# Small products and transposes of a state space preparation, quad by quad or gathered over two quads

## The chip, the cores and the metric

The kernel runs on one core of a Trainium2 chip. The metric is the device time of one execution in microseconds. An execution under the profiler gives, beside its own time, a span (first to last instruction) and the trace from which all rows below are taken. Engines: TensorE (PE, with PEld for its weight loads), VectorE (DVE), ScalarE (ACT), GpSimd (POOL), SyncE (SP).

## The reference

A trunk of two layers on x (256 positions, 2048 wide). Each layer is a token mixer, a cross-attention to 256 memory rows and a squared-ReLU MLP, all with residual adds. The mixer of layer 0 is a gated MLP, that of layer 1 a diagonal complex state space layer, cut here to what matters:

```python
lam = lax.complex(jnp.minimum(lam_re, LAM_RE_MAX), lam_im)      # 128 groups x 64 states
lam_bar = jnp.exp(lam * jnp.exp(log_dt)[:, None])
b_bar = ((lam_bar - 1.0) / lam)[..., None] * bmat                # 64 x 16 per group
bu = jnp.einsum('gpc,bsgc->sbgp', b_bar, u)
_, states = lax.associative_scan(combine, (a, bu), axis=0)       # a = lam_bar at every position
y = jnp.einsum('gcp,sbgp->bsgc', cmat, states).real + d_skip * u
```

The kernel works on chunks of T = 8 positions. For that it needs, for each group, matrices that depend on the parameters alone: the inputs of a chunk to its last state (P), the state to the outputs (Q), and the inputs to the outputs inside a chunk (K). Preparing these is the work that the change touches.

## The kernel before

**The main work.** Nearly all time is matmuls on weights that stream from memory. Every weight tile of 128 x 1024 fp32 values is loaded by SP (`wraw`, 4 buffers), split by ScalarE into a high part (`whi`, line 101) and by VectorE into the rest (`wlo`, line 102), 3 buffers each, and multiplied by TensorE in three passes. In the first MLP, up-projections (lines 163 and 165, 16 matmuls a tile, four tiles to an output, after which lines 168, 169, 545, 101 and 102 make `r`, `hh` and `hl`) alternate with down-projections (lines 579 to 581, 12 matmuls a tile, eight tiles to an output).

**The side work.** `ssm_prep` (from line 672) puts its work as a list of pieces on `self.side`. `tick`, called once per weight tile, takes the next piece off the list at every second tile while the MLP of layer 0 is traced, and gives it a priority 200 instructions behind the main work. A scheduler then orders each engine's queue by priority and by what is ready; at run time each queue is worked off in that order.

**The preparation.** The 128 groups are worked on in 32 quads of four. Each quad has three pieces: `quad` (line 789) loads `b_bc` into `bcq` (3 buffers) and makes `bb` (2 buffers; lines 800 to 802). `quad_q` makes `qt` (lines 810 to 812, 2 buffers), writes it to Qd, multiplies four products of `bb` and `qt` (line 822: 32 x 128 results into one PSUM tile `kp`), and takes the result through `kd` (2 buffers; ScalarE at line 826, VectorE at 827) to Kd by four DMAs (line 830). `quad_p` makes `pq` (lines 810 to 812, one buffer), transposes it in four 128 x 128 pieces (line 838), copies the result to `po` (ScalarE, line 840) and writes it to Pd (line 841). The four products are given to the scheduler with `high_priority(offset=g)`, which puts them at one priority; the transposes have one after the other. PSUM tiles come from `ps`, which alternates between two pools of two banks.

**Behind it.** The mixer of layer 1 reads Pd, Kd and Qd back (line 865), starting at the end of this MLP. All these DMAs stand in POOL's queue.

Of the kernel before, what the change touches and what calls it, by code (L numbers as in the profile page):

```python
# [9 lines left out]
F32 = mybir.dt.float32  # L10
# [3 lines left out]
ALU = mybir.AluOpType  # L14
AX = mybir.AxisListType

P = 128
# [14 lines left out]
T = 8  # L32
# [6 lines left out]
class Trunk:  # L39
# [632 lines left out]
    def ssm_prep(self, pool):  # L672
# [6 lines left out]
        nc, a = self.nc, self.a  # L679
        v = nc.vector  # L680
        W = [P, P]
        NL = 2 * T - 1
# [7 lines left out]
        dsk = pool.tile([P, G // 4], F32, name="dsk", bufs=1)  # L690
        eye = pool.tile([P, 16], F32, name="eye", bufs=1)
# [3 lines left out]
        e = {}  # L695
# [88 lines left out]
        def cols(q):  # L784

            g0 = 32 * (q // 8) + q % 8
            return slice(g0, g0 + 25, 8)

        def quad(q):
            bcq = pool.tile([P, 4, 4, 16], F32, name="bcq", bufs=3)  # L790
            nc.gpsimd.dma_start(out=bcq, in_=a["b_bc"][q])
            v.tensor_scalar(out=bcq[:, 2:4], in0=bcq[:, 2:4], scalar1=sg[:, 0:1], scalar2=None, op0=ALU.mult)
            B1, C2, B2, C1 = (bcq[:, i] for i in range(4))
            bb = pool.tile([P, 4, 2, 16], F32, name="bb", bufs=2)
            tq = pool.tile([P, 4, T + 1, 16], F32, name="tq")
            tb = tq.rearrange("p a b c -> p (a b c)")[:, 0:64].rearrange("p (a c) -> p a c", a=4)
            f1 = F[:, 0, cols(q)].unsqueeze(2).broadcast_to([P, 4, 16])
            f2 = F[:, 1, cols(q)].unsqueeze(2).broadcast_to([P, 4, 16])
            for k, (x1, x2, op) in enumerate(((B1, B2, ALU.subtract), (B2, B1, ALU.add))):
                v.tensor_tensor(out=bb[:, :, k], in0=f1, in1=x1, op=ALU.mult)  # L800
                v.tensor_tensor(out=tb, in0=f2, in1=x2, op=ALU.mult)
                v.tensor_tensor(out=bb[:, :, k], in0=bb[:, :, k], in1=tb, op=op)
            e[q] = bcq, bb, tq

        def times(out, tmp, n, q, x1, x2):
            t1 = T1[:, 0:n, cols(q)].rearrange("p w g -> p g w").unsqueeze(3).broadcast_to([P, 4, n, 16])
            t2 = T2[:, 0:n, cols(q)].rearrange("p w g -> p g w").unsqueeze(3).broadcast_to([P, 4, n, 16])
            b1 = x1.unsqueeze(2).broadcast_to([P, 4, n, 16])
            b2 = x2.unsqueeze(2).broadcast_to([P, 4, n, 16])
            v.tensor_tensor(out=out, in0=t1, in1=b1, op=ALU.mult)  # L810
            v.tensor_tensor(out=tmp, in0=t2, in1=b2, op=ALU.mult)
            v.tensor_tensor(out=out, in0=out, in1=tmp, op=ALU.subtract)

        def quad_q(q):
            bcq, bb, tq = e[q]
            qt = pool.tile([P, T + 1, 4, 16], F32, name="qt", bufs=2)
            times(qt.rearrange("p w g c -> p g w c"), tq, T + 1, q, bcq[:, 3], bcq[:, 1])
            nc.gpsimd.dma_start(out=self.Qd[q // 2][q % 2].rearrange("p r n -> r p n"), in_=qt[:, 1:])
            kp = self.ps([P, T, 16])
            for g in range(4):  # L820
                with self.tc.high_priority(offset=g):
                    nc.tensor.matmul(kp[32 * g:32 * g + 32], bb[:, g], qt[:, 0:T, g, :], start=True, stop=True,
                                     skip_group_check=True)
            kd = pool.tile([P, NL, 16], F32, name="kd", bufs=2)
            nc.gpsimd.memset(kd[:, 0:T - 1, :], 0.0)
            nc.scalar.copy(out=kd[:, T:, :], in_=kp[:, 1:, :])
            v.scalar_tensor_tensor(out=kd[:, T - 1, :], in0=eye, scalar=dsk[:, q:q + 1], in1=kp[:, 0, :],
                                   op0=ALU.mult, op1=ALU.add)
            for t in range(4):
                nc.gpsimd.dma_start(out=self.Kd[q // 2][:, :, q % 2, t], in_=kd[32 * t:32 * t + 16])  # L830

        def quad_p(q):
            bcq, bb, tq = e.pop(q)
            pq = pool.tile([P, 4, T, 16], F32, name="pq")
            times(pq, tq[:, :, 0:T, :], T, q, bb[:, :, 0], bb[:, :, 1])
            pt = self.ps([P, 4, P])
            for g in range(4):
                nc.tensor.transpose(pt[:, g, :], pq[:, g].rearrange("p j c -> p (j c)"), self.ident)
            po = pool.tile([P, 4, P], F32, name="po", bufs=2)
            nc.scalar.copy(out=po, in_=pt)  # L840
            nc.gpsimd.dma_start(out=self.Pd[q // 2][:, q % 2], in_=po)

        sd = self.side
        sd += [poles, bar, zoh]
# [2 lines left out]
        sd += [lambda k=k: power(k) for k in range(5, T + 1)]  # L847
        sd += [lambda: spread(5), last]
        for q in range(G // 4):
            sd += [lambda q=q: quad(q), lambda q=q: quad_q(q), lambda q=q: quad_p(q)]  # L850


    def s5(self, x, cur, nxt):
# [362 lines left out]
```

## Time and profile before

| what | us |
|---|---|
| median of 3 runs (lowest, highest) | 2852.18 (2847.0, 2854.78) |
| the profiled execution's own time | 2848.29 |
| its span | 2846.5 |
| TensorE busy in the span | 2811.6 |
| VectorE busy | 1830.3 |
| ScalarE busy | 1333.4 |
| first and last product of line 822 start at | 791.8 and 1335.5 |
| first and last transpose of line 838 start at | 799.1 and 1344.3 |

A row of the profile names line, engine, operation, output and inputs, shape and count. Matmuls are pipelined: a row's length is longer than the distance to the next start, so costs are read from starts. The waits say which engine waited for which line, the total, the number and the longest.

### The profile page before, as it was taken

The page shows a single profiled execution, that of the slowest core. Times are in us where ns is not written, and L with a number is a line of the kernel's source. Part 1 is how long each engine was busy: PE and PEld are TensorE (multiplying, and loading weights), DVE is VectorE, ACT ScalarE, POOL GpSimd, SP SyncE. Part 2 cuts the span into 40 slices and gives each one's busy share as a digit, 9 for nine tenths or more (in the row PEclk, how much of TensorE's full clock was granted, in tenths as well). Part 3 has the DMA queues.
Part 4 walks back from the last instruction along what each step waited for, and adds up shares of the span by engine and source line. Part 5 has one row for each costly group of instructions (what it writes and reads, how often), then busy time and mean ns, then how long its engine had stood idle before and what let it go on. Part 6 is the DMA issues. An engine that isn't in the chain of part 4 may idle for free.

```text
span 2846.5 us, 39576 instructions
## 1 busy us (share of the span) xinstructions
PE 2811.6 (99%) x15238; PEld 2359.5 (83%) x15238; DVE 1830.3 (64%) x2548; ACT 1333.4 (47%) x1714; POOL 204.0 (7%) x380
## 2 busy tenths in 40 slices
PE   8999999999999999999999999999999999999998
PEld 6888888888888888888777788888888888888886
DVE  6765655585778788787567666555556555565555
ACT  5445544444544444444465445444454444344443
POOL 1000000000022222222011000000000000000000
PEclk9999999999999999999999999999999999999999
DMA  8766655558677777777879766565556666666665
GB/s 288 215 208 200 193 181 177 168 177 241 189 218 226 217 224 219 218 221 218 230 251 275 218 212 207 171 179 180 177 183 192 192 189 188 193 186 192 191 187 154
DMA packets 180461, 579.55 MB, mean 204 GB/s; under 512 B 37440, under 2 KB 39664, under 8 KB 179504
## 3 DMA queue, kind: packets, MB, share of 16 engines
q1 hardware_dynamic: 141440, 511.77, 59.2%
q0 software_dynamic: 38688, 65.19, 8.6%
q8 instruction: 119, 1.95, 0.3%
q14 instruction: 70, 0.57, 0.1%
q10 hardware_dynamic: 144, 0.07, 0.0%
HBM read 553.88 MB, written 22.94 MB: 203 GB/s over the span
## 4 chain that ended last, share of the span: by engine, by line
PE 92%; DMA 3%; DVE 2%; ACT 1%; issue 1%; SPq 0%; POOL 0%; DVEq 0%; ACTq 0%; POOLq 0%
PE acc L163 25%; PE acc L165 13%; PE acc L146 9%; PE acc L145 9%; PE acc L147 9%; PE acc L581 8%; PE acc L580 8%; PE acc L579 8%; PE ps L515 1%; DMA wraw<-in_f_w_down 1%; PE ps L459 1%; DVE wlo L102 1%; PE ps L214 1%; DMA wraw<-in_b_w_in 1%; DMA wraw<-in_f_w_up 1%
## 5 line engine op out<-in xcount | busy, mean ns | idle before, releaser
L102 DVE TENSOR_TENSOR wlo<-wraw,whi 128x1024 fp32r<-128x1024 f32 x952 | 1162.9, 1223 | 842.2 <-ACT whi L101 840.4
L101 ACT CAST whi<-wraw 128x1024 fp32r<-128x1024 f32 x952 | 1001.0, 1052 | 1297.1 <-PE acc L163 402.6
L163 PE MATMUL acc<-act,whi 128*128 128x512 f32 x3072 | 1081.9, 396 | 1.1 <-ACT whi L101 1.1
L165 PE MATMUL acc<-act,wlo 128*128 128x256 f32 x3072 | 864.4, 281 | 0.8 <-DVE wlo L102 0.8
L163 PEld LDWEIGHTS acc<-act,whi 128*128 128x128 f32 x3072 | 575.9, 187 | 133.7 <-issue 1.6
L165 PEld LDWEIGHTS acc<-act,wlo 128*128 128x128 f32 x3072 | 580.3, 189 | 5.2 <-DVE wlo L102 1.8
L145 PE MATMUL acc<-whi,act 128*128 128x512 f32 x1248 | 490.6, 393 | 8.7 <-ACT whi L101 7.2
L146 PE MATMUL acc<-wlo,act 128*128 128x512 f32 x1248 | 488.6, 392 | 5.5 <-DVE wlo L102 5.5
L147 PE MATMUL acc<-whi,act 128*128 128x512 f32 x1248 | 488.0, 391 | 0.3 <-DVE act L102 0.3
L580 PE MATMUL acc<-wlo,hh 128*128 128x512 f32 x992 | 389.5, 393 | 0.5 <-DVE wlo L102 0.4
L579 PE MATMUL acc<-whi,hh 128*128 128x512 f32 x992 | 388.9, 392 | 0.0
L581 PE MATMUL acc<-whi,hl 128*128 128x512 f32 x992 | 388.7, 392 | 0.0
L145 PEld LDWEIGHTS acc<-whi,act 128*128 128x128 f32 x1248 | 235.0, 188 | 58.1 <-ACT whi L101 7.7
L146 PEld LDWEIGHTS acc<-wlo,act 128*128 128x128 f32 x1248 | 235.1, 188 | 55.3 <-DVE wlo L102 8.2
L147 PEld LDWEIGHTS acc<-whi,act 128*128 128x128 f32 x1248 | 235.2, 188 | 48.4 <-DVE act L102 0.7
L580 PEld LDWEIGHTS acc<-wlo,hh 128*128 128x128 f32 x992 | 186.3, 188 | 42.0 <-DVE wlo L102 2.0
L581 PEld LDWEIGHTS acc<-whi,hl 128*128 128x128 f32 x992 | 186.3, 188 | 40.2 <-issue 1.6
L579 PEld LDWEIGHTS acc<-whi,hh 128*128 128x128 f32 x992 | 186.3, 188 | 39.9 <-issue 0.4
L830 POOL DMA_DIRECT2D Kd<-kd x128 | 72.4, 580 | 178.9 <-issue 166.7
L563 DVE SCALAR_TENSOR_TENSOR x<-acc,r,x 128x512 f32<-128x512 f32 x62 | 43.6, 745 | 8.2 <-PE acc L581 8.1
L176 ACT ACTIVATE junk<-x 128x512 f32<-128x512 f32 x56 | 35.3, 630 | 25.8 <-DVE x L556 13.3
L101 ACT CAST hh<-r 128x512 fp32r<-128x512 f32 x64 | 39.5, 617 | 16.7 <-DVE r L545 16.6
(287 smaller groups left out, 1658.0 us busy)
## 6 DMA issues: line engine op xcount, KB each, us to landing
wraw<-in_f_w_up SPq DMA_DIRECT2D x256, 512.0 KB, 4.2
wraw<-in_f_w_down SPq DMA_DIRECT2D x256, 512.0 KB, 4.2
wraw<-in_a_w_in SPq DMA_DIRECT2D x64, 512.0 KB, 4.4
wraw<-in_x_w_q SPq DMA_DIRECT2D x64, 512.0 KB, 3.7
wraw<-in_x_w_k SPq DMA_DIRECT2D x64, 512.0 KB, 3.6
wraw<-in_x_w_v SPq DMA_DIRECT2D x64, 512.0 KB, 3.7
wraw<-in_x_w_o SPq DMA_DIRECT2D x64, 512.0 KB, 3.7
wraw<-in_b_w_out SPq DMA_DIRECT2D x64, 512.0 KB, 4.4
```

Of the source, the lines that this page charges most:

```text
L101: self.nc.scalar.copy(out=hi, in_=src)
L102: self.nc.vector.tensor_tensor(out=lo, in0=src, in1=hi.bitcast(F32), op=ALU.subtract)
L145: nc.tensor.matmul(out[t], ah[:, kt, sl], hi[:, kk, :], start=st, stop=False)
L146: nc.tensor.matmul(out[t], ah[:, kt, sl], lo[:, kk, :], start=False, stop=False)
L147: nc.tensor.matmul(out[t], al[:, kt, sl], hi[:, kk, :], start=False, stop=en)
L163: nc.tensor.matmul(acc[:, f, :], hi[:, kk, sl], both[:, kt].rearrange("p a s -> p (a s)"), start=st, stop=False, skip_group_check=True)
L165: nc.tensor.matmul(acc[:, f, 0:S], lo[:, kk, sl], ah[:, kt, :], start=False, stop=en, skip_group_check=True)
L563: nc.vector.scalar_tensor_tensor(out=xc, in0=acc[:, t, :], scalar=r2[:, t:t + 1], in1=xc, op0=ALU.mult, op1=ALU.add)
L579: nc.tensor.matmul(acc[:, t, :], ah[:, kt % 4, sl], hi[:, kk, :], start=st, stop=False)
L580: nc.tensor.matmul(acc[:, t, :], ah[:, kt % 4, sl], lo[:, kk, :], start=False, stop=False)
L581: nc.tensor.matmul(acc[:, t, :], al[:, kt % 4, sl], hi[:, kk, :], start=False, stop=en)
L830: nc.gpsimd.dma_start(out=self.Kd[q // 2][:, :, q % 2, t], in_=kd[32 * t:32 * t + 16])
```

## The change

The three pieces of a quad become `quad`, `matrices` (`qt` and its write) and `inputs` (`pq`, now with two buffers). After `inputs` of every second quad the same piece also runs `products` for both quads: eight products into one PSUM tile `kp`, then eight transposes into two, all sixteen at one priority, and then the copies and writes of both quads.

```diff
-        def quad_q(q):
-            bcq, bb, tq = e[q]
+        def matrices(q):
+            bcq, bb, tq = e[q]
             qt = pool.tile([P, T + 1, 4, 16], F32, name="qt", bufs=2)
             times(qt.rearrange("p w g c -> p g w c"), tq, T + 1, q, bcq[:, 3], bcq[:, 1])
             nc.gpsimd.dma_start(out=self.Qd[q // 2][q % 2].rearrange("p r n -> r p n"), in_=qt[:, 1:])
-            kp = self.ps([P, T, 16])
-            for g in range(4):
-                with self.tc.high_priority(offset=g):
-                    nc.tensor.matmul(kp[32 * g:32 * g + 32], bb[:, g], qt[:, 0:T, g, :], start=True, stop=True,
-                                     skip_group_check=True)
...
-        def quad_p(q):
-            bcq, bb, tq = e.pop(q)
-            pq = pool.tile([P, 4, T, 16], F32, name="pq")
+        def inputs(q):
+            bb, tq, qt = e[q]
+            pq = pool.tile([P, 4, T, 16], F32, name="pq", bufs=2)
             times(pq, tq[:, :, 0:T, :], T, q, bb[:, :, 0], bb[:, :, 1])
-            pt = self.ps([P, 4, P])
-            for g in range(4):
-                nc.tensor.transpose(pt[:, g, :], pq[:, g].rearrange("p j c -> p (j c)"), self.ident)
...
+        def products(q0):
+            quads = [(q, *e.pop(q)) for q in (q0, q0 + 1)]
+            kp = self.ps([P, 2, T, 16])
+            pts = [self.ps([P, 4, P]) for _ in quads]
+            n = 0
+            for i, (q, bb, qt, pq) in enumerate(quads):
+                for g in range(4):
+                    with self.tc.high_priority(offset=n):
+                        nc.tensor.matmul(kp[32 * g:32 * g + 32, i], bb[:, g], qt[:, 0:T, g, :], start=i == 0,
+                                         stop=True, skip_group_check=True)
+                    n += 1
+            for (q, bb, qt, pq), pt in zip(quads, pts):
+                for g in range(4):
+                    with self.tc.high_priority(offset=n):
+                        nc.tensor.transpose(pt[:, g, :], pq[:, g].rearrange("p j c -> p (j c)"), self.ident)
+                    n += 1
+            for i, (q, *_) in enumerate(quads):
+                kd = pool.tile([P, NL, 16], F32, name="kd", bufs=2)
+                nc.gpsimd.memset(kd[:, 0:T - 1, :], 0.0)
+                nc.scalar.copy(out=kd[:, T:, :], in_=kp[:, i, 1:, :])
+                v.scalar_tensor_tensor(out=kd[:, T - 1, :], in0=eye, scalar=dsk[:, q:q + 1], in1=kp[:, i, 0, :],
+                                       op0=ALU.mult, op1=ALU.add)
+                for t in range(4):
+                    nc.gpsimd.dma_start(out=self.Kd[q // 2][:, :, q % 2, t], in_=kd[32 * t:32 * t + 16])
+            for (q, *_), pt in zip(quads, pts):
+                po = pool.tile([P, 4, P], F32, name="po", bufs=2)
+                nc.scalar.copy(out=po, in_=pt)
+                nc.gpsimd.dma_start(out=self.Pd[q // 2][:, q % 2], in_=po)
...
-            sd += [lambda q=q: quad(q), lambda q=q: quad_q(q), lambda q=q: quad_p(q)]
+            sd += [lambda q=q: quad(q), lambda q=q: matrices(q), lambda q=q: inputs(q)]
+            if q % 2:
+                last_piece = sd.pop()
+                sd += [lambda q=q, f=last_piece: (f(), products(q - 1))]
```

How the scheduler orders TensorE's queue with this can be read from the built programs. Before, in the second quad (the products of a quad, then its transposes between the down-projection's matmuls):

```order
L580 MATMUL acc_7051<-wlo_7073,hh_5584 128x512
L822 MATMUL ps_6735<-qt_6730,bb_6686 32x128 x4
L581 MATMUL acc_7051<-whi_7072,hl_5585 128x512
...
L579 MATMUL acc_7051<-whi_7120,hh_5911 128x512
L838 MATMUL ps_6788<-ident_84,pq_6784 128x128
L580 MATMUL acc_7051<-wlo_7121,hh_5911 128x512
L838 MATMUL ps_6788<-ident_84,pq_6784 128x128
L581 MATMUL acc_7051<-whi_7120,hl_5912 128x512
```

After, in the fifth pair, at the end of an up-projection (line 837 are the products, 843 the transposes; `bb_7804` and `pq_7912` are of the pair's first quad, `bb_7972` and `pq_8080` of its second):

```order
L843 MATMUL ps_8085<-ident_84,pq_7912 128x128 x4
L165 MATMUL acc_8292<-act_4834,wlo_8373 128x256
L163 MATMUL acc_8292<-act_4834,whi_8372 128x512
...
L837 MATMUL ps_8084<-qt_7863,bb_7804 32x128
L843 MATMUL ps_8086<-ident_84,pq_8080 128x128 x4
L837 MATMUL ps_8084<-qt_7863,bb_7804 32x128 x3
L837 MATMUL ps_8084<-qt_8024,bb_7972 32x128 x4
L579 MATMUL acc_8402<-whi_8405,hh_7447 128x512
```

The first quad's transposes stand in a row; a few large matmuls later come one product, the second quad's transposes in a row, and the other seven products in a row. It is so in all 16 pairs.

VectorE's queue at the same pair, after the change (line 849 is what 827 was; `wlo_8406` and `wlo_8424` belong to the two tiles that TensorE works on behind the pair's products):

```order
L102 TENSOR_TENSOR wlo_8406<-wraw_8403,whi_8405 128x1024 [waits DMAHW1_49,PE_49,Activation_49]
L102 TENSOR_TENSOR wlo_8424<-wraw_8421,whi_8423 128x1024 [waits DMAHW2_49,PE_49,Activation_49]
L800 TENSOR_TENSOR bb_8172<-F_5579,bcq_8169 128x4x16 [waits PE_49]
L800 TENSOR_TENSOR bb_8172<-F_5579,bcq_8169 128x4x16
L102 TENSOR_TENSOR wlo_8487<-wraw_8484,whi_8486 128x1024 [waits DMAHW3_49,Activation_49]
L169 TENSOR_TENSOR r_8291<-acc_8292,r_8291 128x512 [waits Activation_49]
L849 SCALAR_TENSOR_TENSOR kd_8103<-eye_5576,dsk_5575,ps_8084 128x16 [waits DMASW5_49,DMASW0_49,Activation_49]
```

The first operation on the next pair's `bb` waits for TensorE, since its buffer is the one that the products above read; before, it waited for the products of the quad before the last.

ScalarE's queue at that place, after the change (848 is what 826 was, 855 what 840 was):

```order
L101 CAST whi_8486<-wraw_8484 128x1024 [waits DMAHW3_49,DVE_49,PE_49]
L168 COPY r_8291<-acc_8292 128x512 [waits PE_49]
L848 COPY kd_8103<-ps_8084 128x112 [waits DMASW5_49,DMASW6_49,DMASW0_49,DMASW7_49,PE_49,Pool_49]
L855 COPY po_8122<-ps_8086 128x512 [waits DMASW4_49]
L848 COPY kd_8111<-ps_8084 128x112 [waits DMASW2_49,DMASW3_49,DMASW1_49,DMASW4_49,DVE_49,Pool_49]
L101 CAST hh_8185<-r_8291 128x512 [waits DVE_49]
L101 CAST whi_8504<-wraw_8502 128x1024 [waits DMAHW4_49,PE_49,Activation_49]
```

The copies of both quads' `kd` and the second `po` stand together here, and the second copy out of `ps_8084` waits for VectorE; before, one `kd` copy stood here for each quad, out of a bank of its own.

More of the change, by code (lines that the diff above doesn't have):

```diff
@@ L818, in quad_q @@
             nc.gpsimd.dma_start(out=self.Qd[q // 2][q % 2].rearrange("p r n -> r p n"), in_=qt[:, 1:])
-            kp = self.ps([P, T, 16])
-            for g in range(4):
-                with self.tc.high_priority(offset=g):
-                    nc.tensor.matmul(kp[32 * g:32 * g + 32], bb[:, g], qt[:, 0:T, g, :], start=True, stop=True,
-                                     skip_group_check=True)
-            kd = pool.tile([P, NL, 16], F32, name="kd", bufs=2)
-            nc.gpsimd.memset(kd[:, 0:T - 1, :], 0.0)
@@ L826, in quad_q @@
[L826 to L830, printed above, removed]
-        def quad_p(q):
-            bcq, bb, tq = e.pop(q)
-            pq = pool.tile([P, 4, T, 16], F32, name="pq")
-            times(pq, tq[:, :, 0:T, :], T, q, bb[:, :, 0], bb[:, :, 1])
-            pt = self.ps([P, 4, P])
-            for g in range(4):
[L838 to L841, printed above, removed]
+            e[q] = bb, tq, qt
@@ new lines, in inputs @@
+        def inputs(q):
+            bb, tq, qt = e[q]
+            pq = pool.tile([P, 4, T, 16], F32, name="pq", bufs=2)
+            times(pq, tq[:, :, 0:T, :], T, q, bb[:, :, 0], bb[:, :, 1])
+            e[q] = bb, qt, pq
+        def products(q0):
[26 more added lines that the diff above has]
+                nc.gpsimd.dma_start(out=self.Pd[q // 2][:, q % 2], in_=po)
```

## Prediction

> **What bounds the kernel now.** I read the page's first lines, then the chain that ended last, and then the stretch in which the prepared work runs.
>
> ```profile
> span 2846.5 us, 39576 instructions
> PE 2811.6 (99%) x15238; PEld 2359.5 (83%) x15238; DVE 1830.3 (64%) x2548; ACT 1333.4 (47%) x1714; POOL 204.0 (7%) x380
> PE 92%; DMA 3%; DVE 2%; ACT 1%; issue 1%; SPq 0%; POOL 0%; DVEq 0%; ACTq 0%; POOLq 0%
> ...
> 770.00:1345.00 575.00, 575.00 (x3123) 476.23 (x3122) 465.70 (x742) 255.14 (x314) 138.81 (x250) 1.00 0.74 218
> ```
>
> TensorE is on the path 92% of the time. In the stretch of the first MLP that holds all 32 quads (770 to 1345 us; the columns are length, then busy time of PE, weight loads, DVE, ACT, POOL) it is never idle, at a granted clock of 1.00. So an operation there costs what it pushes the next large matmul back. VectorE is busy for 465.7 of 575 us, 81%: it is the engine that could become late. I therefore need two things: the price of small matmuls between large ones, and VectorE's margin.
>
> **What the small work costs now.** The first fence has one quad's products, the second its transposes one by one, the third four transposes in a row (start, length).
>
> ```profile
> 791.23 0.39 PE L579 MATMUL acc<-whi,hh 128*128 128x512 f32 x1
> 791.45 0.39 PE L580 MATMUL acc<-wlo,hh 128*128 128x512 f32 x1
> 791.77 0.43 PE L822 MATMUL ps<-qt,bb 128*32 128x128 f32 x8
> 792.13 0.50 PE L581 MATMUL acc<-whi,hl 128*128 128x512 f32 x1
> 792.46 0.39 PE L579 MATMUL acc<-whi,hh 128*128 128x512 f32 x1
> ```
>
> ```profile
> 819.41 0.39 PE L579 MATMUL acc<-whi,hh 128*128 128x512 f32 x1
> 819.64 0.27 PE L838 MATMUL ps<-ident,pq 128*128 128x128 f32 x1
> 819.67 0.48 PE L580 MATMUL acc<-wlo,hh 128*128 128x512 f32 x1
> ...
> 820.72 0.48 PE L580 MATMUL acc<-wlo,hh 128*128 128x512 f32 x1
> 821.03 0.39 PE L581 MATMUL acc<-whi,hl 128*128 128x512 f32 x1
> 821.26 0.39 PE L579 MATMUL acc<-whi,hh 128*128 128x512 f32 x1
> ```
>
> ```profile
> 868.92 0.39 PE L163 MATMUL acc<-act,whi 128*128 128x512 f32 x1
> 869.15 0.28 PE L165 MATMUL acc<-act,wlo 128*128 128x256 f32 x1
> 869.27 0.60 PE L838 MATMUL ps<-ident,pq 128*128 128x128 f32 x4
> 869.63 0.48 PE L163 MATMUL acc<-act,whi 128*128 128x512 f32 x1
> 869.94 0.28 PE L165 MATMUL acc<-act,wlo 128*128 128x256 f32 x1
> ```
>
> Large matmuls start 0.227 us apart (791.23 to 791.45, less rounding). From 791.45 to 792.46 there are two such steps, 0.454, but 1.01 us passed: a quad's products cost 0.556 us. The four are eight rows, since each fp32 product takes two passes. Most of the price is not work: the first product starts 0.32 us behind a large matmul instead of 0.227, and the last of the eight (start 791.77 + 0.43 - 0.27, its own length) is followed only 0.20 us later by a large one, which then takes a step of 0.33 instead of 0.227.
>
> Four single transposes: 819.41 to 821.26 is 1.85 us for six large steps (1.362), so 0.49 us. Four in a row: 869.15 to 869.94 is 0.79 us for steps of 0.117 and 0.230, so 0.44 us. The trace has both kinds and mixtures; I take the middle, 0.465. In all: 32 x 0.556 + 32 x 0.465 = 17.8 + 14.9 = 32.7 us.
>
> **What they cost after the change.** The order shows, in each of the 16 pairs of quads, four transposes in a row, some large matmuls, and then one block: one product, four transposes, seven products. The products are not in one run; the lone one costs a change of shape into and out of the transposes. The prices of such changes stand in the later state space stage (L919, L967, L973 are products on 32 columns, L935 transposes):
>
> ```profile
> 1458.11 1.88 PE ps L919 x64
> ...
> 1492.81 1.09 PE L935 MATMUL ps<-ident,z 128*128 128x128 f32 x8
> 1493.66 0.47 PE L145 MATMUL acc<-whi,act 128*128 128x512 f32 x1
> ...
> 1528.42 1.03 PE L935 MATMUL ps<-ident,z 128*128 128x128 f32 x8
> 1529.38 0.64 PE L967 MATMUL ps<-dq,us 128*32 128x128 f32 x16
> ```
>
> 64 rows in 1.88 us are sixteen passes of four: (1.88 - 0.27) / 15 = 0.107 us a pass. Eight transposes behind other transposes need 7 x 0.109 to their last start (869.27 to 869.63 gives that step), so from 1528.42 the last starts at 1529.18 and the product 0.20 later. Behind products, 1492.81 to 1493.66 is 0.85 where seven steps and the 0.03 to the large matmul are 0.79: the first step there takes 0.06 more. Products to transposes I take as products to a large matmul, 0.20.
>
> The block, from the start of the last large matmul ahead to the second one behind: 0.32 in; 0.13 for the lone product's two passes (0.16 for four products, less three issue steps); 0.20 to the transposes; 0.38 for their steps (0.166 + 2 x 0.109); 0.20 back; 0.37 for seven products (0.16 + 2 x 0.107); 0.20 out; 0.33 for the first large step. Together 2.13, less the two ordinary steps 0.454: 1.68 us. With the other four transposes, 0.44, a pair costs 2.12 us; now it costs 2 x (0.556 + 0.465) = 2.04. So **+0.08 us a pair, +1.3 us in all**. The bounds: if the lone product with its two changes (0.13 + 0.20 + 0.06) cost nothing, 16 x (0.08 - 0.39) = -5 us; if the two changes at the transposes each cost as much as one to a large matmul and back (0.09 + 0.11 more), 16 x 0.28 = +4.5 us. I take +1.3, since each step in it has a row.
>
> **VectorE and ScalarE.** The elementwise work is the same in number and size; it moves. These are the waits in the stretch, then the groups that VectorE's queue is made of:
>
> ```profile
> DVE wlo L102 <- ACT whi L101: 59.6, 54, 1.9
> DVE bcq L792 <- DMA bcq<-in_b_bc: 24.1, 17, 4.0
> DVE pq L810 <- PE ps L838: 9.9, 13, 1.1
> DVE bb L800 <- PE ps L822: 8.2, 12, 1.2
> ...
> PEld acc L165 <- DVE wlo L102: 0.6, 2, 0.3
> ```
>
> ```profile
> L102 DVE TENSOR_TENSOR wlo<-wraw,whi 128x1024 fp32r<-128x1024 f32 x197 | 240.2, 1220 | 60.2 <-ACT whi L101 59.6
> L811 DVE TENSOR_TENSOR tq<-T,bcq 128x576 f32<-128x576 f32 x32 | 24.2, 757 | 0.9
> L812 DVE TENSOR_TENSOR qt<-qt,tq 128x576 f32<-128x576 f32 x32 | 24.1, 754 | 0.5
> L810 DVE TENSOR_TENSOR pq<-T,bb 128x512 f32<-128x512 f32 x32 | 22.0, 687 | 9.9 <-PE ps L838 9.9
> ```
>
> VectorE waits for TensorE in two places now (9.9 and 8.2 us) and for the b_bc loads (24.1 us, once 4.0), and TensorE paid only 0.6 us for all of it, because its weights are two to three tiles ahead. With a second pq buffer the 9.9 us can go: worth nothing, as nobody waited. The bb wait grows: the first bb of a pair overwrites a buffer that all products of the pair before have to have read, and in VectorE's queue it stands behind two splits that TensorE has not used yet. Behind the wait comes a whole pair's work. In the up-projection, from the bb wait to the end of the sixth split behind it, I count 6 splits at 1.14 (their spacing; the group's mean is 1.22, with overlap), 4 operations at 0.75, 4 at 0.69, 11 small ones at 0.22, two quick ones on kd and six on r and hl at 0.6: 19.1 us. TensorE needs that split seven tiles after the block; a tile is 8 x (0.230 + 0.117) = 2.78 us, so 19.4 us. It is a tie with 0.3 us to spare in perhaps half of the pairs; in the down-projection there is less elementwise work and some 1.5 us to spare. I cost it at nothing, with bounds of 0 and, if VectorE's work comes out 5 to 10% longer (1 to 2 us, less the 0.3), 8 x 0.7 to 8 x 1.7 = 6 to 14 us.
>
> The later Kd and Pd writes are the same in number; now ten of them are issued together. Behind the last ones on POOL stand the first loads of the state space stage:
>
> ```profile
> 1337.72 2.27 POOL L830 DMA_DIRECT2D Kd<-kd  x4 [12.11 <-DVE kd L827]
> 1345.66 0.57 POOL L841 DMA_DIRECT2D Pd<-po  x1 [5.67 <-ACT po L840]
> 1346.21 2.13 POOL L865 DMA_DIRECT2D pq<-Pd  x4
> ```
>
> Eight Kd issues at 0.57 us push these loads back by about 5 us; their first use is the L919 row at 1458, so this costs nothing.
>
> **Forecast.** 2848.29 us (span 2846.5 and 1.8 around it) + 1.3 = 2849.6 for a run like the profiled one. That one lies 3.9 us under the median shown; against the median it is 2852.18 + 1.3 = **2853.5 us**, no measurable change.
>
> **Rivals.**
> *Faster: the products run together.* If the lone product joins the other seven, a pair needs one block of products (0.556 + 2 x 0.107 = 0.77) and two runs of transposes (0.88): 1.65 instead of 2.04, 16 x -0.39 = -6 us, 2846 us. That is what the change says it does. The order of TensorE's rows speaks against it in every pair. Beyond 0.3% (8.6 us, about what a measurement of this kernel tells from no change) it would also need idle time to vanish, of which there is hardly any. 5%.
>
> *Slower: the splits come late behind the block.* Both quads' products now lie in one PSUM bank. ScalarE copies the first half, VectorE reads it, and only then ScalarE may copy the second half; the next tile's cast stands behind that copy. VectorE reaches its read after the bb work, a split and an operation on r: 0.35 + 1.14 + 0.6 + 0.2 = 2.3 us. Then copy, hh and cast (0.25 + 0.62 + 1.05) bring whi to 4.2 us and, in VectorE's queue, wlo to some 6.3 us, needed at three tiles, 8.2. So it decides only when 1.9 us are lost there, or 0.3 us at the sixth split. A loss of 1 to 1.5 us in half of the pairs is 8 to 12 us: 2862 to 2865. For it speaks the tie; against it that VectorE lost 4 us at once before and TensorE lost 0.3. 17%.
>
> The Trainium skill (PSUM — Partial Sum Buffer, section on PSUM bank collisions) says that two engines must not be in one bank and 32-partition quadrant at the same time, and that software therefore orders ScalarE against VectorE too. By that rule the hand-over just described is there and is all of this rival's first part; without it the second copy would follow the first at once and the forecast would lose this rival, not a microsecond of its sum. The trace of before has a bank per quad, so no row here shows it.
>
> **Chances and range.** Same (within 0.3%) 0.78, slower 0.17, faster 0.05. The range takes in the -5 of the bounds with the spread of the runs shown (2847.0 to 2854.78) and reaches up to the slower case: 2846 to 2864.
>
> **What would show it.** Right: in the timeline of a pair four transposes, then one product row of two, four transposes, and fourteen rows of products, with 1.6 to 1.75 us lost; products and transposes together near 34 us. Wrong on TensorE: a lone product with no gap to the transposes. Wrong on VectorE: waits of the weight loads for wlo of more than a few us in all, at 860 to 960 us or 1045 to 1140 us above all; or b_bc waits longer than 4 us.

## The result and the profile after

The changed kernel takes 2884.94 us (median of 5, 2880.08 to 2888.72) against 2850.17 for the kernel before (median of 5): a ratio of 1.0122, with a 95% interval of 1.011 to 1.0135. It is 35 us slower, where 2853.5 was forecast, and outside the stated range.

First the lines of the page after that answer to those of before, then the row of the windows for 770 to 1345 us (its columns are explained in the prediction):

```profile
span 2878.3 us, 39497 instructions
PE 2821.2 (98%) x15238; PEld 2370.9 (82%) x15238; DVE 1817.8 (63%) x2548; ACT 1336.1 (46%) x1714; POOL 202.8 (7%) x380
...
770.00:1345.00 575.00, 551.18 (x2927) 458.61 (x2927) 425.85 (x702) 241.22 (x294) 126.76 (x231) 0.98 0.68 206
```

The span is 31.8 us longer. In the stretch in which TensorE was never idle, it is now busy for 551.2 of 575 us, and its granted clock is 0.98 instead of 1.00. VectorE did not become the fuller engine: 425.9 us instead of 465.7, with 702 of its operations in the stretch instead of 742. So something makes both wait. The waits of 770 to 1400 us name it:

```profile
DVE bcq L792 <- DMA bcq<-in_b_bc: 60.4, 16, 7.1
...
DVE bb L800 <- PE ps L837: 17.7, 9, 2.4
...
PE acc L165 <- DVE wlo L102: 15.5, 5, 3.7
...
ACT kd L848 <- DVE kd L849: 10.5, 11, 1.4
...
PE acc L580 <- DVE wlo L102: 8.3, 2, 4.6
```

VectorE's wait for the `b_bc` load grew from 24.1 to 60.4 us, the longest from 4.0 to 7.1; and TensorE, which had lost 0.6 us to `wlo` between 770 and 1345 us, now waits seven times between 1.9 and 4.6 us. One of the seven, engine by engine. TensorE (line 580 needs the `wlo` of its tile):

```profile
836.87 0.39 PE L579 MATMUL acc<-whi,hh 128*128 128x512 f32 x1
841.86 0.80 PE L580 MATMUL acc<-wlo,hh 128*128 128x512 f32 x1 [4.60 <-DVE wlo L102]
842.45 0.63 PE L581 MATMUL acc<-whi,hl 128*128 128x512 f32 x1
842.88 0.63 PE L579 MATMUL acc<-whi,hh 128*128 128x512 f32 x1
```

VectorE, with that `wlo` in its last row:

```profile
832.41 0.22 DVE L802 TENSOR_TENSOR bb<-bb,tq 128x64 f32<-128x64 f32 x1
839.72 0.29 DVE L792 TENSOR_SCALAR bcq<-bcq,sg 128x128 f32<-128x128 f32 x1 [7.09 <-DMA bcq<-in_b_bc]
...
840.59 1.22 DVE L102 TENSOR_TENSOR wlo<-wraw,whi 128x1024 fp32r<-128x1024 f32 x1
```

GpSimd, which issues the load (the bracket is its idle time before the row):

```profile
818.99 0.57 POOL L856 DMA_DIRECT2D Pd<-po  x1 [32.95 <-ACT po L855]
821.07 0.55 POOL L856 DMA_DIRECT2D Pd<-po  x1 [1.51 <-ACT kd L848]
822.69 4.53 POOL L852 DMA_DIRECT2D Kd<-kd  x8 [1.07 <-issue]
827.14 0.90 POOL L819 DMA_DIRECT2D Qd<-qt  x1
...
828.10 0.65 POOL L791 DMA_DIRECT2D bcq<-in_b_bc  x1
```

Read from the bottom up: the load is issued at 828.10, and VectorE's first use of it starts at 839.72, 11.6 us later. Ahead of it stand ten stores (two of Pd, eight of Kd) and then, with only a memset between it and the load, the write of Qd. VectorE works its queue off in order, so the split of `wlo` at 840.59 stands behind that first use. The rows of the kernel before have the load ahead of Qd:

```profile
804.72 0.54 POOL L791 DMA_DIRECT2D bcq<-in_b_bc  x1 [2.83 <-DVE tq L811]
806.53 0.85 POOL L818 DMA_DIRECT2D Qd<-qt  x1 [1.27 <-DVE qt L812]
```

What each place costs stands in the table of DMA issues for 770 to 1345 us (the last number is the median from issue to landing); the kernel before, then after:

```profile
Qd<-qt POOLq DMA_DIRECT2D x32, 256.0 KB, 12.1
...
bcq<-in_b_bc POOLq DMA_DIRECT2D x29, 128.0 KB, 3.3
```

```profile
Qd<-qt POOLq DMA_DIRECT2D x30, 256.0 KB, 11.9
...
bcq<-in_b_bc POOLq DMA_DIRECT2D x29, 128.0 KB, 5.8
```

A write of Qd takes 12 us in both kernels. Before, every load was issued 0.5 to 2.8 us ahead of the next write of Qd, and none of the 29 took more than 5.0 us. After, 11 of the 29 were issued 0.9 to 1.0 us behind one; these took 10.6 to 12.6 us, and each landed 0.2 to 0.8 us after that write. In three pairs of the same trace the ten stores stand ahead of the load and Qd behind it (the loads at 974.54, 1018.68 and 1244.39); these loads took 3.9, 4.1 and 4.8 us. The first of them, with its Qd issued only at 977.27:

```profile
969.84 4.62 POOL L852 DMA_DIRECT2D Kd<-kd  x8 [1.00 <-DVE r L545]
...
974.54 0.65 POOL L791 DMA_DIRECT2D bcq<-in_b_bc  x1
```

So the stores alone do not make a load late; the write of Qd does.

**The account of the 31.8 us**, from the starts of the large matmuls: seven stalls, 24.9 us beyond the ordinary steps; another 10 us behind five of them, where steps take 0.43 instead of 0.227 us at a granted clock of 0.50 (last section); 1.4 us more for products and transposes (34.15 us instead of 32.72, summed over all rows); less some 2 us of small waits of before that are gone, and 2.7 us that come back in the state space stage (there the lag behind the kernel before falls from 34.5 to 31.8 us, where it stays). These add up to 31.6.

### The profile page after: what moved, and what is told of

Its sections match the earlier page's. It is cut to its first block, busy times and chain, and to the rows that moved or that the text cites. A ratio compares the mean times of both kernels' runs of the same rounds, so it can differ in the third digit from the quotient of the medians.

```text
span 2878.3 us, 39497 instructions
## 1 busy us (share of the span) xinstructions
PE 2821.2 (98%) x15238; PEld 2370.9 (82%) x15238; DVE 1817.8 (63%) x2548; ACT 1336.1 (46%) x1714; POOL 202.8 (7%) x380
## 5 line engine op out<-in xcount | busy, mean ns | idle before, releaser
L792 DVE TENSOR_SCALAR bcq<-bcq,sg 128x128 f32<-128x128 f32 x32 | 9.4, 294 | 60.4 <-DMA bcq<-in_b_bc 60.4
```

## The experiments

Three theories. **A**: the load stands behind the 12 us write of Qd in GpSimd's DMA queue; it lands late, and VectorE stands still with weight splits queued behind. **B**: VectorE is late because of the block itself (the bb wait, both quads' products in one PSUM bank); the wait for the load is a symptom. **C**: the load is late because it is issued late. All ratios are to the kernel before, on the same chip: its median was 2849.94 us beside the two runs that move the load or Qd to SyncE, the fourth buffer and the first run of products, and 2850.27 beside the other four.

### The load on another queue

```diff
-            nc.gpsimd.dma_start(out=bcq, in_=a["b_bc"][q])
+            nc.sync.dma_start(out=bcq, in_=a["b_bc"][q])
```

> The changed kernel (2885 us, kernel before 2850) with the loads of b_bc issued by SyncE instead of GpSimd, nothing else. Theory A (the load stands behind the 12 us write of Qd in GpSimd's DMA queue, lands 11 to 12 us late, and VectorE waits for it with weight splits queued behind): the loads land in 2 to 5 us, no wait for bcq over 4 us, no stall of TensorE over 1 us in this stage, 2850 to 2854. Theory B (VectorE is late because of the block itself: bb wait, one PSUM bank for both copies; the waits for the load are a symptom): seven stalls stay, 2875 or more. Theory C (the load is issued late, because GpSimd waits with the stores of Pd): also 2850 to 2854, so this run does not part A from C.

Measured: 2850.19 us, ratio 1.000 (0.9991 to 1.0009). One line takes back the whole loss. The windows, the DMA issues and the waits:

```profile
770.00:1345.00 575.00, 575.00 (x3110) 480.90 (x3109) 456.63 (x742) 258.01 (x312) 117.46 (x212) 1.00 0.73 218
```

```profile
bcq<-in_b_bc SPq DMA_DIRECT2D x29, 128.0 KB, 4.1
```

```profile
DVE bb L800 <- PE ps L837: 20.4, 11, 2.4
DVE bcq L792 <- DMA bcq<-in_b_bc: 11.8, 10, 2.3
...
PEld acc L580 <- DVE wlo L102: 1.2, 2, 0.8
PE acc L580 <- DVE wlo L102: 0.4, 1, 0.4
```

TensorE is busy for all 575 us again. The bb wait is longer than in the changed kernel (20.4 against 17.7 us) and costs TensorE nothing. So B falls; A and C are not told apart. Seven of the 29 loads took 5.1 to 7.1 us, more than expected, without harm. The edit also moves the loads in time: on SyncE they do not wait for GpSimd's stores, and none is issued earlier than 4.9 us behind a write of Qd. The one that was issued at 828.10 is now issued at 827.03, 3.1 us ahead of its Qd.

### The write of Qd on another queue, the load left where it is

```diff
-            nc.gpsimd.dma_start(out=self.Qd[q // 2][q % 2].rearrange(...), in_=qt[:, 1:])
+            nc.sync.dma_start(out=self.Qd[q // 2][q % 2].rearrange(...), in_=qt[:, 1:])
```

> The changed kernel with only the write of Qd issued by SyncE; the load of b_bc keeps its place in GpSimd's queue, behind the stores of Pd and Kd. A: the load, issued as late as now, lands in 2 to 5 us instead of 11 to 12; the stalls go; 2850 to 2856. C: the late issue decides, so waits and stalls stay: 2875 to 2885. B: 2875 or more.

Measured: 2850.43 us, ratio 1.0005 (0.9996 to 1.0013). The load still stands behind both Pd and all eight Kd:

```profile
821.07 4.52 POOL L852 DMA_DIRECT2D Kd<-kd  x8 [1.08 <-issue]
...
826.05 0.59 POOL L791 DMA_DIRECT2D bcq<-in_b_bc  x1 [0.26 <-issue]
```

It is issued 2.05 us earlier than in the changed kernel and takes 5.5 us instead of 11.6. So most of the 8 us gained is the landing, as A says, and a smaller part the issue. C alone does not hold: the ten stores ahead stayed. The landing of Qd itself is not recorded on SyncE, so it is not shown whether that write became shorter there.

### The load ahead of Qd in the same queue

```diff
-            nc.gpsimd.dma_start(out=bcq, in_=a["b_bc"][q])
+            with self.tc.high_priority(offset=400):
+                nc.gpsimd.dma_start(out=bcq, in_=a["b_bc"][q])
```

> The changed kernel with nothing on another queue: only the priority of the b_bc load is raised by 400 instructions, so that in GpSimd's own queue it stands among the Kd stores and ahead of the write of Qd that it stood behind. A (12 us landing behind Qd): the loads that stood right behind a Qd land in 3 to 6 us, no stall over 1 us, 2850 to 2856. If it is GpSimd's queue as such that is too slow with ten stores at once (C), the loads come out as late as now within 3 us, and stalls stay: 2865 or more.

Measured: 2852.05 us, ratio 1.0003 (0.9994 to 1.0013), though every transfer is still on GpSimd:

```profile
822.87 1.74 POOL L853 DMA_DIRECT2D Kd<-kd  x3 [1.07 <-issue]
824.57 0.63 POOL L792 DMA_DIRECT2D bcq<-in_b_bc  x1
825.16 3.00 POOL L853 DMA_DIRECT2D Kd<-kd  x5
828.15 0.84 POOL L820 DMA_DIRECT2D Qd<-qt  x1
```

That load took 3.3 us. The order within the queue is enough; GpSimd is not too slow. Four other loads, issued 3.5 to 5.8 us behind a Qd, still took 7.4 to 9.5 us, more than expected, without harm.

### A fourth buffer for the load

```diff
-            bcq = pool.tile([P, 4, 4, 16], F32, name="bcq", bufs=3)
+            bcq = pool.tile([P, 4, 4, 16], F32, name="bcq", bufs=4)
```

> The changed kernel with four buffers for b_bc instead of three. A: the load and its first use on VectorE move one quad ahead together and the load still stands behind Qd, so it changes nothing: 2878 to 2890. C (issue too late, the buffer comes free too late): the stalls go, 2850 to 2856. B: no change, 2878 to 2890.

Measured: 2885.74 us, ratio 1.0133 (1.0115 to 1.015): the loss stays in full. The load is issued at 828.69, still next behind Qd, and its first use moved ahead by a quad with it:

```profile
DVE bcq L792 <- DMA bcq<-in_b_bc: 58.3, 15, 7.2
```

### The products of two quads in one run, with the loads on SyncE

On the kernel before: `quad_q` of every second quad gives all eight products at one priority into one tile, and each quad's transposes get one priority of their own, so that TensorE's order is four transposes, eight products, four transposes, with large matmuls between.

```diff
-            kp = self.ps([P, T, 16])
-            for g in range(4):
-                with self.tc.high_priority(offset=g):
+            e["r"] = e.get("r", []) + [(q, bb, qt)]
+            if q % 2:
+                rows(e.pop("r"))
+        def rows(quads):
+            kp = self.ps([P, 2, T, 16])
...
+                    with self.tc.high_priority(offset=n):
...
             for g in range(4):
-                nc.tensor.transpose(pt[:, g, :], ...)
+                with self.tc.high_priority(offset=g):
+                    nc.tensor.transpose(pt[:, g, :], ...)
...
-            nc.gpsimd.dma_start(out=bcq, in_=a["b_bc"][q])
+            nc.sync.dma_start(out=bcq, in_=a["b_bc"][q])
```

> The kernel before with the eight products of two quads in one run at one priority, each quad's four transposes at one priority by themselves, and the b_bc loads on SyncE. By the prices read before: a pair pays 0.77 for the products and 2 x 0.44 for the transposes, 1.65 instead of 2.04 us; 16 x 0.39 = 6 us under the kernel before, 2843 to 2847, if VectorE keeps pace (A). B: stalls of several us as in the changed kernel, 2870 or more, since eight results in one bank come at once here too.

Measured: 2848.28 us, ratio 0.9996 (0.9987 to 1.0005): no change that shows, and a little over the expected 2843 to 2847. Summed over all rows, products and transposes cost 26.7 us instead of 32.7, the 6 us that were worked out; but TensorE stalled twice, for 2.4 and 2.3 us. The load issued on SyncE at 827.04 took 8.2 us. It stands behind 512 KB weight loads there, and it was also issued 4.4 us behind a write of Qd; which of the two made it late is not shown:

```profile
835.24 0.29 DVE L792 TENSOR_SCALAR bcq<-bcq,sg 128x128 f32<-128x128 f32 x1 [5.70 <-DMA bcq<-in_b_bc]
```

### The same run of products, all transfers on GpSimd

The kernel of the run above with `nc.gpsimd` for the load again.

> The kernel before with the eight products of two quads in one run and every transfer left on GpSimd's queue. A: one load of each pair stands behind a write of Qd again, lands in 11 to 12 us, and VectorE waits 4 to 7 us for it; TensorE saves 6 us on small matmuls and loses some 20 to 35 in stalls: 2860 to 2880. If the stalls come from the elementwise work of two quads being pushed together and not from the load, they would have shown with the loads on SyncE too (there 4.7 us in all), so this run should then be at 2845 to 2850.

Measured: 2912.34 us, ratio 1.0214 (1.0198 to 1.0229). The cause was made again in another program, and the slowdown came, larger than expected: twelve stalls instead of seven, 47.9 us, and 13 of the 29 loads took 9.9 us or more.

```profile
823.68 0.83 POOL L818 DMA_DIRECT2D Qd<-qt  x1
...
824.64 0.57 POOL L791 DMA_DIRECT2D bcq<-in_b_bc  x1
```

```profile
834.82 0.28 DVE L792 TENSOR_SCALAR bcq<-bcq,sg 128x128 f32<-128x128 f32 x1 [6.84 <-DMA bcq<-in_b_bc]
```

### The same run, with Qd on SyncE

```diff
-            nc.gpsimd.dma_start(out=self.Qd[q // 2][q % 2].rearrange(...), in_=qt[:, 1:])
+            nc.sync.dma_start(out=self.Qd[q // 2][q % 2].rearrange(...), in_=qt[:, 1:])
```

> The kernel before with the eight products of two quads in one run, and only the writes of Qd on SyncE. A with the prices as read: loads land in 3 to 5 us, small matmuls 26.6 instead of 32.6 us, 2843 to 2847. The writes of Qd on SyncE cost some 4 us at the loads of the next stage (as in the changed kernel with Qd there), which would make it 2846 to 2850.

Measured: 2858.06 us, ratio 1.0033 (1.0022 to 1.0044): 8 us over the higher of the two times expected. In the profiled execution (2868.27 us, 10 over the median) TensorE stalls four times in this stage, 9.8 us in all, the longest 5.3 us at 941, and once more for 3.1 us at its end (1397). Around the longest a write of Qd stands between weight loads on SyncE (issued at 925.29), and ScalarE waits for a weight tile:

```profile
936.55 1.06 ACT L101 CAST whi<-wraw 128x1024 fp32r<-128x1024 f32 x1 [3.71 <-DMA wraw<-in_f_w_up]
```

VectorE also waits 6.7 us for a `b_bc` load there:

```profile
945.07 0.29 DVE L792 TENSOR_SCALAR bcq<-bcq,sg 128x128 f32<-128x128 f32 x1 [6.65 <-DMA bcq<-in_b_bc]
```

The split that TensorE waits for starts right behind this row, at 945.27, and TensorE goes on at 946.55. So the longest stall ends with the load; the weight tile had come 8.5 us earlier. The causes of the other three were not told apart.

### The same run, with the loads on ScalarE's queue

```diff
-            bcq = pool.tile([P, 4, 4, 16], F32, name="bcq", bufs=3)
-            nc.gpsimd.dma_start(out=bcq, in_=a["b_bc"][q])
+            bcq = pool.tile([P, 4, 4, 16], F32, name="bcq", bufs=4)
+            nc.scalar.dma_start(out=bcq, in_=a["b_bc"][q])
```

> The kernel before with the eight products of two quads in one run, the b_bc loads on ScalarE's own queue and four buffers for them. A with the prices as read: loads land in 2 to 4 us, no stall over 1 us in this stage, 2842 to 2846. If the issue on ScalarE holds up its casts (it waits for a buffer of VectorE's), a stall of the weight loads for whi shows and it is 2850 or more.

Measured: 2846.69 us, ratio 0.9986 (0.9976 to 0.9996): 0.14% under the kernel before, the fastest of this study, and just over the expected 2842 to 2846. Products and transposes cost 26.7 us, 6 less than before, and the median is 3.6 us lower; no run has the loads on ScalarE's queue without the run of products, so that the 3.6 us come from the 6 is argued and not shown; the loads took 2.2 to 7.0 us, more than expected, and TensorE's longest stall is 1.0 us.

## Why the prediction was wrong

**TensorE's part was right.** The pair came out as drawn: four transposes, a product of two rows, four transposes, fourteen rows.

```profile
817.48 0.60 PE L843 MATMUL ps<-ident,pq 128*128 128x128 f32 x4
...
818.83 0.39 PE L579 MATMUL acc<-whi,hh 128*128 128x512 f32 x1
819.15 0.41 PE L837 MATMUL ps<-qt,bb 128*32 128x128 f32 x2
819.49 0.66 PE L843 MATMUL ps<-ident,pq 128*128 128x128 f32 x4
820.07 0.64 PE L837 MATMUL ps<-qt,bb 128*32 128x128 f32 x14
820.64 0.50 PE L580 MATMUL acc<-wlo,hh 128*128 128x512 f32 x1
820.98 0.39 PE L581 MATMUL acc<-whi,hl 128*128 128x512 f32 x1
```

From 818.83 to 820.98 it is 2.15 us, 1.70 beyond two ordinary steps; the sum said 2.13 and 1.68. With the loads out of the way (on SyncE), products and transposes cost 34.2 us instead of 32.7 (worked out: 34.0), and the ratio is 1.000. What was forecast is the changed kernel without its load behind Qd.

**The step that failed** is the one on the later Kd and Pd writes. It asked only what stands behind the last of them, found loads that are used 110 us later, and said "this costs nothing". But the same stores stand ahead of a `b_bc` load in 14 pairs, on the same queue, in 11 of them the write of Qd has slipped in between, and that load has a user at once: it takes 10.6 to 12.6 us, VectorE waits up to 7.1 us for it, and TensorE stalls seven times. The rows quoted for that step were three of GpSimd's queue at the end of the stage; the order of the load against Qd in each pair was not looked at. The trace of before held the two times, 12.1 us for Qd and 3.3 us for a load ahead of it, though no load directly behind a Qd.

**VectorE's tie did not decide.** The forecast's slower rival put the loss on the bb wait or on the hand-over of the PSUM bank, 8 to 12 us. The side was right, the mechanism and size were not. The bb wait did grow (8.2 to 17.7 us), and with the loads on SyncE it grew to 20.4 without a stall. The hand-over is there too: ScalarE waits 10.5 us in all, 1.4 at the longest, for VectorE between its two copies of `kp`. That agrees with the rule of the Trainium skill (PSUM — Partial Sum Buffer, section on PSUM bank collisions) that was cited. It set nothing back: with the loads on SyncE the two engines still share the bank, and TensorE has no stall.

**The range** took its upper end from that rival, so it could not hold a cause that the working did not have. The last sentence of the working did name its sign: `b_bc` waits longer than 4 us came, up to 7.1.

**The faster rival** was priced about right: products in one run save the 6 us that were worked out, and with the loads on ScalarE's queue the median is 3.6 us under the kernel before. The change itself did not put them in one run.

## What to carry to other kernels

A change that gathers stores moves the loads that share their queue. For every transfer ask what stands directly ahead of it in its queue before and after, and how long that one takes to land, and then how soon the load's first user stands on its engine. A deeper buffer did not help here, where the scheduler moved the user ahead together with the load. Taking the two apart did: the load ahead of the write in the same queue, or one of the two on another queue.

## What the runs showed of the hardware

**A short load issued behind a slow write can land as late as the write, on another queue too.** Behind Qd, a 128 KB load that takes 3.3 us takes 11.6, and lands within 0.8 us after it. The Trainium skill (DMA: Bandwidth & Descriptors, section on queues, rings and completion order) says that descriptors of one ring are consumed in order (it says so of the queues of SyncE and ScalarE), while an engine goes round between queues. The late landing on one queue fits the first half. But with the loads on SyncE and Qd on GpSimd, 14 of the 29 loads were issued while a Qd was in flight (19 in the changed kernel), and nine of the 14 also landed 0.2 to 1.1 us after it. Issued 4.4 to 5.0 us behind a Qd, loads took 6.5, 6.8 and 8.7 us on its own queue (the changed kernel and its like with all transfers on GpSimd) and 6.1 to 8.2 us on SyncE's or ScalarE's (three of these five landed before their Qd). So with the loads on SyncE it counts above all that none is issued right behind a Qd. With Qd on SyncE and the load on GpSimd, nine loads issued 0.3 to 2.6 us behind a Qd took 4.6 to 7.1 us. How much the shared queue adds by itself, and why a Qd holds up a load of another queue, is open.

**After most stalls TensorE's clock was halved.** The stall at 836.87 shows it above: behind 4.60 us of idle time the steps are 0.43 us (842.45 to 842.88) instead of 0.227. Two of the other six, by the first matmul behind each with its idle time, and four windows of 3.41 us around them (the second number is TensorE's busy time, the third from the end the granted clock):

```profile
884.63 0.39 PE L165 MATMUL acc<-act,wlo 128*128 128x256 f32 x1 [2.84 <-DVE wlo L102]
...
1065.31 0.39 PE L165 MATMUL acc<-act,wlo 128*128 128x256 f32 x1 [3.50 <-DVE wlo L102]
```

```profile
882.62:886.03 3.41, 1.40 (x8) 1.26 (x9) 3.41 (x6) 0.00 (x0) 0.56 (x1) 1.00 0.14 24
886.03:889.45 3.42, 3.42 (x13) 2.84 (x12) 3.42 (x6) 2.58 (x3) 0.83 (x1) 0.50 0.64 195
1060.11:1063.53 3.42, 1.70 (x10) 1.19 (x8) 0.37 (x2) 1.04 (x1) 0.00 (x0) 1.00 0.10 41
1063.53:1066.94 3.41, 1.64 (x10) 1.46 (x11) 3.41 (x5) 0.00 (x0) 1.28 (x2) 1.00 0.39 83
```

Idle for 2.84 us brought half the clock, idle for 3.50 us and for 1.91 us (the stall that ends at 918.30) did not; the three not shown (3.48, 3.70 and 3.73 us) did. Length alone does not decide. In each of these traces every change of the granted clock falls on one grid of 3.41 us, and the clock follows the idle time inside one of its windows. The stall of 2.84 us left 2.01 us idle in one window, and the next one has a clock of 0.50. The stall of 3.50 us lies across two windows, with 1.72 and 1.77 us idle, and the clock stays at 1.00. In the ten traces, from 700 to 1400 us, all 21 windows at full clock with 1.96 us idle or more were followed by half the clock, and none with 1.78 us or less; between 1.84 and 1.91 us it went both ways. The Trainium skill (TensorE: Matmul & The Clock Gate, Part 1) says that the gate watches free-running windows of about 3.4 us. The trace agrees, with 3.41 us; the 2 us are what these ten traces show.
